# Recording both mixers of a two-layer encoder and ordering them with one list planner for all engines

## The chip, the cores and the metric

The kernel is one program on one NeuronCore of a Trainium2 chip. The metric is the device time of one execution in microseconds (us), lower is better. The engines named below are PE (TensorE matmul), DVE (VectorE), ACT (ScalarE), POOL (GpSimd) and SP (SyncE, which issues most weight loads). Each engine runs its own instructions in order and waits on semaphores for the others.

## The reference, cut to what matters

512 tokens of width 1024 go through two layers. Each layer is a mixer, a cross-attention to 256 memory tokens and a gated convolutional FFN; the mixers are what this case is about.

```python
# layer 0
proj = xn @ w_in                                   # 1024 -> 3080 columns
fox  = forgetting_attention(fq, fk, fv, log_f)     # 8 heads of 64: causal softmax(q k / 8 + F_q - F_k) v
diff = differential_attention(q1, q2, k1, k2, v)   # 4 heads: (softmax_1 - lam * softmax_2) v, chunk-causal
mixed = concat(fox, rms_norm(diff) * 0.8) @ w_out
x = x + mixed;  x = x + memory_cross_attention(...);  x = x + conv_ffn(...)
# layer 1
qk = silu(causal_conv(proj_qk));  h = mlstm_chunkwise(q, k, v, i, log_f)   # 4 heads, q/k 128, v 256
mixed = (rms_norm(h) * sigmoid(og)) @ w_out
x = x + mixed;  ...;  y = rms_norm(x)
```

## The kernel before, in words

Activations lie transposed in eight tiles of 128 x 512 (`x0` to `x7`). Almost every product is made in three passes (`mm3`, L388 to L390): both factors are split into a high and a low part, and high x high, high x low and low x high are summed in PSUM. So each weight block of 128 x 1024 is loaded by SP into a `raw` tile, cast by ACT to `wh` and subtracted by DVE to `wl`; three such sets of buffers rotate. One projection block is 24 matmuls of 512 columns. Four PSUM banks (`acc0` to `acc3`) hold projections, two `s` and two `w` banks hold scores, transposes and attention sums.

`mix0` writes the first mixer as items. A differential head is a q and a k projection (`p_qk`), eight score blocks with softmax (`p_soft`, L798 and L799: a matmul pair, a DVE reduction `sm`, an ACT exponential, a DVE reciprocal), transposes (`p_turn`, L831), a sum over values (`weigh`, L844), and an RMS norm whose per-token roots go through DRAM and back as a broadcast row (`p_far_norm`: POOL computes `y`, issues `roots<-y`, then `hrb<-roots`). A fox pair (two heads of 64) does the same with two heads side by side (`weigh`, L1068, 64 columns each); its bias rows come from `decays`, a running sum of the log forget gates that DVE and ACT compute, POOL sends to DRAM and then spreads over 128 partitions (`fb<-decays`); POOL masks them (`tb<-fb`). `p_memory` prepares the memory tokens for the cross-attention, `p_fill` computes blocks of its keys early, into a bank that stays held until the next stage, and `p_out` is the output projection, eight blocks over the eight mixed tiles.

`mix1` is the mLSTM likewise: gates (two scans, logs and exponentials on four rows), two value projections, and for each of four heads a q and a k block with a convolution of four taps and a tanh, two output gates, four score blocks, the row sums (`dens`, L2254), the sums over values (`nums`, L2275) and the norm.

Two planners stand in the file. `Plan` keeps one clock for PE and rough clocks for ACT and DVE: each item has a PE duration, a priority, resources and a `chain` of rough durations behind it. It picks the ready item of the lowest priority number and calls its function, which issues all of the item's instructions, those of DVE, ACT, POOL and SP among them, in that order. Both mixers are ordered by `Plan` alone: the instructions then go to the framework in the order of issue, and the framework, which knows their dependencies, orders each engine's list. `Sched` is finer: every instruction of every engine is a task with a duration, a latency, ring buffers that it takes and frees, and a due time; the engine with the earliest possible start goes next. `rest` (cross-attention and FFN of a layer) is ordered by `Sched`, and there `planned(True, 4)` chains the instructions of DVE, ACT, POOL and SP each to the one before by an ordering edge without a semaphore, so that the planned order is the order on the engine. All instructions of DVE, ACT, POOL and SP go through the helper at L310 and carry that line.

Of the kernel before, what the change touches and what calls it, by code (L numbers as in the profile page):

```python
# [31 lines left out]
DECAY_AT = 90.0  # L32
MEM_AT, MEM_STEP = (140.0, 100), (24.0, 16.0)
FILLS, FILL_AT, FILL_PRIO = 2, (210.0, 140.0), 99
# [41 lines left out]
class Item:  # L76
    def __init__(self, fn, dur, deps, prio, take, free, chain, pre, after, order, load, st):
# [8 lines left out]
class Plan:  # L86
# [11 lines left out]
    def add(self, fn, dur=0.0, deps=(), prio=None, take=(), free=(), chain=(), pre=(), after=0.0, order=(), load=(), st=None, soon=False):  # L98
        it = Item(fn, dur, [d for d in deps if d is not None], len(self.items) if prio is None else prio, take, free, chain, pre, after, order, load, st)
        it.n, it.soon = len(self.items), soon  # L100
        self.items.append(it)
        return it

    def run(self):
        todo = sorted(self.items, key=lambda i: (i.prio, i.n))
        eng, t = self.eng, self.t
        while todo:
# [27 lines left out]
            for e, d in pick.pre:  # L135
                eng[e] = max(eng[e], t - 4.0) + d
            t += pick.dur
# [28 lines left out]

class Task:
    def __init__(self, eng, dur, fn, deps, prio, take, free, lat, after):
        self.after = after
        self.eng, self.dur, self.fn, self.prio, self.lat = eng, dur, fn, prio, lat  # L170
        self.deps = [d for d in deps if d is not None]
        self.take, self.free = take, free
        self.end = None


WAIT = {"DVE": 0.4, "ACT": 0.3}
ONE, TWO, FORM, THEN = 4, 12, 10.0, (2, 1, 1)
OUT = (0, 4, 1, 5, 2, 6, 3, 7)

class Sched:  # L180
# [3 lines left out]
    def __init__(self, wait={}, **res):  # L184
        self.tasks, self.wait, self.held, self.ahead = [], wait, [], AHEAD
# [16 lines left out]
    def dues(self):  # L202
# [6 lines left out]
        for r, s in self.slots.items():  # L209
            takes = [(t, st) for t in self.tasks for q, st in t.take if q == r]  # L210
            if r == "acc":
                takes = [(None, st) for st in self.held] + takes
# [22 lines left out]

    def run(self):
        if self.wait:
            self.dues()
# [5 lines left out]
        for t in self.tasks:  # L244
            for r, _ in t.take:
                want[r].append(t)
# [3 lines left out]
        while any(todo.values()):  # L250
            best = None
            for e, ts in todo.items():
                able = []
                for t in ts[:120]:
                    at = max(t.after, -99.0 if e == "-" else now[e])
                    ok = True
                    for d in t.deps:
# [3 lines left out]
                        at = max(at, d.end + (0.0 if d.eng == e else d.lat))  # L261
                    if not ok:
                        continue
                    for j, (r, _) in enumerate(t.take):
                        if want[r][0] is not t:
# [14 lines left out]
            if e == "PE":  # L280
                idle += at - now[e]
            t.start, t.end = at, at + t.dur
            now[e] = t.end
            for r, st in t.take:
                want[r].pop(0)
# [10 lines left out]

class InOrder:
# [3 lines left out]
    def __init__(self, tc, engine):  # L301
        self.tc, self.engine = tc, engine
# [3 lines left out]
    def __getattr__(self, name):  # L306
        issue = getattr(self.engine, name)

        def call(*a, **k):
            i = issue(*a, **k)  # L310
# [7 lines left out]
    def follow(self, after=None):  # L318
        self.next = after or True


class Engines:
    def __init__(self, tc, names):
        self.nc = tc.nc
        self.chains = [InOrder(tc, getattr(tc.nc, n)) for n in names]
# [10 lines left out]

class Builder:
    def __init__(self, tc, t):
        self.tc, self.nc, self.t = tc, Engines(tc, ORDERED), t
# [12 lines left out]
    def til(self, pool, tag, shape=(P, 512), dtype=F32, bufs=None):  # L352
        return pool.tile(list(shape), dtype, tag=tag, name=self.nm(tag), bufs=bufs or 2)

# [47 lines left out]
    def p_proj(self, pl, src, xs, evac, chain, deps=(), kdeps=None, edeps=(), prio=None, n=SEQ, nk=KB8, order=None, etake=(), per=2, eorder=(), load=()):  # L402
# [5 lines left out]
        for c, e in zip(cuts, cuts[1:] + [nk]):  # L408
# [12 lines left out]
            for k in ks:  # L421
# [4 lines left out]
                pre=(("A", 0.12 * nk), ("D", 0.14 * nk)) if first else (), st=st,  # L426
            )
        return pl.add(lambda: evac(st["ps"]), 0, [last, *edeps], prio, take=etake, free=("acc",), chain=chain, order=eorder, load=load, st=st, soon=True)
# [92 lines left out]
    def p_out(self, pl, src, mixed, kdeps, gain, gi, order, prio, reload=False, order0=None):  # L521
# [3 lines left out]
        for m in range(KB8):  # L525
            e = self.p_proj(
                pl, src[m], mixed, lambda ps, m=m: self.xadd(m, ps, reload), (("D", 0.6),), kdeps=kdeps, order=order, prio=prio + m
# [192 lines left out]
    def split_rows(self, pool, *rows):  # L720

        t = pool.tile([P, SEQ], F32R, name=self.nm("rows"))
# [50 lines left out]
    def p_qk(self, pl, dq, dk, par, kdeps, edeps, prio):  # L773

        st = {}
        q = self.p_proj(
            pl, dq, self.xs, lambda ps: st.update(q=self.q_parts(ps)), (("D", 0.66), ("A", 0.52), ("D", 0.6), ("D", 0.6)), load=(("A", 0.52),),
# [3 lines left out]
            pl, dk, self.xs, lambda ps: st.update(k=self.k_parts(ps, par)), (("D", 0.6), ("A", 0.52), ("D", 0.6), ("D", 0.6)), load=(("A", 1.56),),  # L781
# [64 lines left out]

    def p_values(self, pl, src, edeps, prio, kdeps=None, ready=None):
# [28 lines left out]
    def mix0(self):  # L876
        nc, t, tc = self.nc, self.t, self.tc
        with tc.tile_pool(name="mix0", bufs=1, reuse_waits="tile") as mp:
            self.mp = mp
            self.kbt = [[mp.tile([P, 512], F32R, name=f"kb{s}{i}") for i in range(2)] for s in range(2)]  # L880
# [4 lines left out]
            sub8 = self.warm[:, 2:3]  # L885
            dmask = mp.tile([P, 512], F32, name="dmask")
            nc.vector.memset(dmask[:], 0.0)
            nc.vector.memset(dmask[0:64, 448:512], BIG)
            mh, ml = ([None if k in (2, 3) else mp.tile([P, SEQ], F32R, name=f"{n}{k}") for k in range(8)] for n in ("mh", "ml"))
# [4 lines left out]
            self.x = [self.xp.tile([P, SEQ], F32, name=f"x{k}", tag=f"x{k}") for k in range(KB8)]  # L894
# [74 lines left out]
            for h in range(4):  # L969
                p = 10 + 10 * h  # L970
                if h == 0:
                    v, ve = self.p_values(pl, t["dv"], [norm], p - 1, xk, [lambda: vw[1:], second])
                st, qk = self.p_qk(pl, t["dq"][h], t["dk"][h], h % 2, xk, [norm], p)
                pt = {}
                got = pl.add(lambda pt=pt: pt.update(t=self.til(mp, "pt", (P, 1536), bufs=3)), 0, qk, p + SOFT_PRIO, take=("pt",))
                ss, ts = [], []
                for i in range(4):
                    n = P * (i + 1)
                    bias = lambda n=n: dmask[:, 512 - n : 512]
                    r1, a1, b1 = self.p_soft(pl, st, 0, i, bias, qk, p + SOFT_PRIO)  # L980
                    r2, a2, b2 = self.p_soft(pl, st, 1, i, bias, qk, p + SOFT_PRIO)
# [9 lines left out]
                    c = pl.add(both, 0, [b1, b2], p + SOFT_PRIO, free=("e",), chain=(("D", 0.08), ("A", 0.1 + 0.45 * n / 512), ("D", 0.07 + 0.6 * n / 512)))  # L991
                    ss += [a1, a2]
                    ts.append(self.p_turn(pl, r1, i, pt, [c, got], p + SOFT_PRIO))
                pl.add(lambda: None, 0, ss, p + SOFT_PRIO, free=("qk",))
# [9 lines left out]
                w = pl.add(weigh, 2.14, ts + ve, p + SOFT_PRIO, take=("w", "ta"), free=("w", "pt"), chain=(("A", 0.5),))  # L1004
                used.append(w)
                if h == 3:
                    pl.add(lambda: None, 0, used, p + SOFT_PRIO, free=("v",))
                w = pl.add(lambda: None, 0, [w], p + SOFT_PRIO, chain=(("A", 0.52),))
# [6 lines left out]
                f = self.p_far_norm(pl, sq, 1.0 / P, EPS, (mp, "hrb", (P, SEQ), F32, 1), scaled, [w], p + SOFT_PRIO, chain=(("D", 0.66),), late=LATE)  # L1015
                kd[4 + h] = [pl.add(lambda: None, 0, [f], p + SOFT_PRIO, free=("ta",), chain=(("A", 0.52), ("D", 0.6)))]


            for p_ in range(4):
                p = 50 + 10 * p_  # L1020
                if p_ == 0:
                    v, ve = self.p_values(pl, t["fv"], [norm], p - 1, xk)
                    used = []
                st, qk = self.p_qk(pl, t["fq"][p_], t["fk"][p_], p_ % 2, xk, [norm], p)
# [3 lines left out]
                for s in range(2):  # L1028
# [9 lines left out]
                    got = pl.add(lambda pt=pt: pt.update(t=self.til(mp, "pt", (P, 1536), bufs=3)), 0, qk, p + SOFT_PRIO, take=("pt",))  # L1038
                    items.append((h, s, pt, fb, b, got, []))
                for i in range(4):  # L1040
                    n = P * (i + 1)
                    for h, s, pt, fb, b, got, ts in items:
# [8 lines left out]
                        r1, a1, b1 = self.p_soft(pl, st, s, i, bias, qk + [b], p + SOFT_PRIO)  # L1051
# [5 lines left out]
                        c = pl.add(norm1, 0, [b1], p + SOFT_PRIO, chain=(("D", 0.13 + 0.27 * n / 512),))  # L1057
                        ss.append(a1)
                        ts.append(self.p_turn(pl, r1, i, pt, [c, got], p + SOFT_PRIO))
                pl.add(lambda: None, 0, ss, p + SOFT_PRIO, free=("qk", "fb", "fb"))  # L1060
                def weigh(p_=p_, pts=[i[2] for i in items], v=v):
# [16 lines left out]
                    pl.add(weigh, 2.4, ts + ve, p + SOFT_PRIO, take=("w",), free=("w", "pt", "pt"), chain=(("A", 0.5), ("D", 0.6)))  # L1078
                )
                used += kd[p_]  # L1080
                if p_ == 3:
                    pl.add(lambda: None, 0, used, p + SOFT_PRIO, free=("v",))
            self.p_memory(pl, 0, MEM_AT[0], MEM_STEP[0], [g])
            self.p_fill(pl, 0, FILL_AT[0], FILL_PRIO, FILLS)
            self.p_out(pl, t["wo0"], lambda: (mh, ml), kd, "xat", 0, [4, 5, 6, 7, 0, 1, 2, 3], 100, True, self.memnorm)
            pl.run()
            self.plan = pl
# [52 lines left out]
    def p_fill(self, pl, layer, after, prio, blocks):  # L1140

        self.fills = []
        for b in range(blocks):
            st = {}
            last = None
            for m in (2 * b, 2 * b + 1):
                for k in range(0, KB8, 4):

                    def fn(m=m, k=k, st=st):
                        if k == 0:  # L1150
                            st["w"] = self.weight(self.t["xk"][layer, m])
                            if m % 2 == 0:
                                st["ps"] = self.acc_bank(st["banks"][0])
                        (wh, wl), (xh, xl) = st["w"], self.mems()
# [9 lines left out]
                        pre=(("A", 0.95), ("D", 1.14)) if first else (), st=st,  # L1164
# [937 lines left out]
    def mix1(self):  # L2102
        nc, t, tc = self.nc, self.t, self.tc
        H = 4
        with tc.tile_pool(name="mix1", bufs=1, reuse_waits="tile") as mp:
            self.mp = mp
            pl = Plan(s=2, w=2, at=2, q=2, wt=3)
# [391 lines left out]
```

## Time and profile before

| | us |
|---|---|
| median of 3 runs | 1406.71 |
| lowest, highest run | 1405.83, 1407.87 |
| the profiled execution, its device time | 1407.05 |
| its span from first to last instruction | 1404.9 |
| PE busy, DVE busy, ACT busy, POOL busy | 1390.2, 1186.4, 874.4, 146.8 |

The stages follow each other: the first mixer until about 255 us, the rest of layer 0 until about 680, the second mixer until about 932, the rest of layer 1 and the final norm until the end. A PE row in the timeline gives the start of a matmul and its modelled length. Matmuls are pipelined, so that the next one starts before the modelled end of the one before; the distance between two starts tells more than the busy time. The granted TensorE clock is 1.000 over the whole run.

### The profile page before, as it was taken

What the parts mean: (1) busy time and instruction counts of PE and PEld (TensorE: products, weight loads), DVE (VectorE), ACT (ScalarE), POOL (GpSimd) and SP (SyncE); (2) the same over time, 40 slices, a digit from 0 to 9 for tenths busy, and PEclk for the clock granted to TensorE, in tenths of its full rate; (3) what the DMA queues carried; (4) which work ended last, traced back from release to release, by engine and by line L of the source; (5) the groups of instructions that cost most, each with busy time, mean ns of one, the idle gap of its engine ahead of it and who ended that gap; (6) DMA issues with size and microseconds to landing.
All of it is one profiled execution on the core that took longest, in us unless ns stands there. A gap on an engine that the chain in (4) does not pass through costs nothing.

```text
span 1404.9 us, 23512 instructions
## 1 busy us (share of the span) xinstructions
PE 1390.2 (99%) x8876; PEld 1265.2 (90%) x8876; DVE 1186.4 (84%) x2042; ACT 874.4 (62%) x1486; POOL 146.8 (10%) x213
## 2 busy tenths in 40 slices
PE   9999999999999999999999999999999999999998
PEld 8888878899899999999888888989989999999997
DVE  7787786888799999999768876678878999999984
ACT  6797565666576665666456664456656866565555
POOL 0002230010011111011001120001000111110000
PEclk9999999999999999999999999999999999999999
DMA  6225324765567787674333332367464878776522
GB/s 207 91 53 154 117 68 151 246 188 158 158 145 191 211 199 187 151 200 106 86 108 105 129 98 83 120 188 240 136 185 114 196 201 204 182 185 168 154 66 81
DMA packets 80544, 211.06 MB, mean 150 GB/s; under 512 B 8640, under 2 KB 8640, under 8 KB 80432
## 3 DMA queue, kind: packets, MB, share of 16 engines
q1 hardware_dynamic: 63520, 165.02, 36.3%
q0 software_dynamic: 15904, 43.44, 17.7%
q8 instruction: 69, 1.13, 0.3%
q10 hardware_dynamic: 1008, 1.12, 0.2%
q14 instruction: 43, 0.35, 0.1%
HBM read 203.20 MB, written 6.34 MB: 149 GB/s over the span
## 4 chain that ended last, share of the span: by engine, by line
PE 85%; DVE 8%; ACT 3%; issue 2%; DMA 1%; POOL 1%; SPq 0%; POOLq 0%; DVEq 0%; ACTq 0%
PE acc L388 16%; PE acc L390 16%; PE acc L389 16%; PE w L388 4%; PE w L389 4%; PE w L390 4%; PE s L388 3%; PE s L390 3%; PE s L389 3%; PE acc L451 2%; PE acc L452 2%; PE acc L450 2%; DVE wl L310 1%; DVE qc L310 1%; PE w L2275 1%
## 5 line engine op out<-in xcount | busy, mean ns | idle before, releaser
L310 ACT CAST wh<-raw 128x1024 fp32r<-128x1024 f32 (+2 forms) x217 | 222.0, 1026 | 160.9 <-PE acc L389 76.4
L310 DVE TENSOR_TENSOR wl<-raw,wh 128x1024 fp32r<-128x1024 f32 (+2 forms) x217 | 259.6, 1198 | 39.2 <-ACT wh L310 37.9
L388 PE MATMUL acc<-xh,wh 128*128 128x256 f32 (+1 forms) x704 | 228.7, 325 | 0.0
L390 PE MATMUL acc<-xh,wl 128*128 128x256 f32 (+1 forms) x704 | 227.4, 323 | 0.5 <-DVE wl L310 0.5
L389 PE MATMUL acc<-xl,wh 128*128 128x256 f32 (+1 forms) x704 | 227.1, 323 | 0.0
L390 PEld LDWEIGHTS acc<-xh,wl 128*128 128x128 f32 x704 | 134.4, 191 | 9.3 <-DVE wl L310 0.9
L388 PEld LDWEIGHTS acc<-xh,wh 128*128 128x128 f32 x704 | 134.5, 191 | 7.6
L389 PEld LDWEIGHTS acc<-xl,wh 128*128 128x128 f32 x704 | 134.5, 191 | 7.5
L310 DVE SCALAR_TENSOR_TENSOR qc<-va,vec,qc 128x512 f32<-128x512 f32 x176 | 131.8, 749 | 6.9 <-ACT qc L310 4.0
L389 PE MATMUL acc<-f,k 128*128 128x256 f32 x336 | 92.5, 275 | 0.0
L390 PE MATMUL acc<-f,k 128*128 128x256 f32 x336 | 92.5, 275 | 0.0
L388 PE MATMUL acc<-f,k 128*128 128x256 f32 x336 | 92.5, 275 | 0.0
L310 ACT ACTIVATE qc<-va,vec 128x512 f32<-128x512 f32 x88 | 71.1, 812 | 19.2 <-DVE q L310 9.5
L388 PE MATMUL w<-q,wh 128*128 128x512 f32 x208 | 79.1, 380 | 0.6 <-ACT qc L310 0.6
L390 PE MATMUL w<-q,wl 128*128 128x512 f32 x208 | 78.9, 379 | 0.0
L389 PE MATMUL w<-q,wh 128*128 128x512 f32 x208 | 78.9, 379 | 0.0
L310 ACT ACTIVATE u<-acc 128x256 f32<-128x256 f32 x96 | 36.4, 379 | 68.1 <-PE acc L390 66.4
L390 PE MATMUL acc<-mem,wl 128*128 128x256 f32 (+1 forms) x236 | 73.8, 313 | 1.1 <-DVE wl L310 1.1
L388 PE MATMUL acc<-mem,wh 128*128 128x256 f32 (+1 forms) x236 | 73.9, 313 | 0.1
L389 PE MATMUL acc<-mem,wh 128*128 128x256 f32 (+1 forms) x236 | 73.7, 312 | 0.0
L310 DVE TENSOR_TENSOR x<-acc,x 128x512 f32<-128x512 f32 (+1 forms) x43 | 28.0, 653 | 47.2 <-PE acc L390 47.2
L310 ACT CAST k<-xe 128x512 fp32r<-128x512 f32 x84 | 51.0, 614 | 25.4 <-DVE xe L310 10.7
(414 smaller groups left out, 4207.0 us busy)
## 6 DMA issues: line engine op xcount, KB each, us to landing
raw<-in_up_dram SPq DMA_DIRECT2D x46, 512.0 KB, 4.3
raw<-in_down_dram SPq DMA_DIRECT2D x32, 512.0 KB, 4.6
sa<-in_up_dram SPq DMA_DIRECT2D x28, 512.0 KB, 5.1
sa<-in_up_dram POOLq DMA_DIRECT2D x28, 512.0 KB, 6.5
vb<-in_up_dram SPq DMA_DIRECT2D x42, 256.0 KB, 4.0
xe<-in_up_dram POOLq DMA_DIRECT2D x42, 256.0 KB, 4.8
raw<-in_wo_dram SPq DMA_DIRECT2D x16, 512.0 KB, 3.6
raw<-in_xk_dram SPq DMA_DIRECT2D x16, 512.0 KB, 3.9
```

Of the source, the lines that this page charges most:

```text
L310: i = issue(*a, **k)
L388: mm(out, wh, xh, start=first, stop=False, skip_group_check=parts)
L389: mm(out, wh, xl, start=False, stop=False, skip_group_check=parts)
L390: mm(out, wl, xh, start=False, stop=last, skip_group_check=parts)
L450: mm(ps, xh[k][:, ts], wh, start=(k == 0), stop=False)
L451: mm(ps, xh[k][:, ts], wl, start=False, stop=False)
L452: mm(ps, xl[k][:, ts], wh, start=False, stop=(k == 7))
L2275: nc.tensor.matmul(ps[:, lo:], vv[s][:, c], a[:], start=(s == 0), stop=(s == 3))
```

## The change

The items of both mixers still go through `Plan.run`, but their instructions are no longer issued there. A `Recorder` stands in front of the engines: each call becomes a `Task` of `Sched`, with a duration from a table by engine, operation and size (`cost`), with dependencies worked out from the tiles that it reads and writes (`Ref`, `View`, `touch`), and with the ring buffers of its tiles. The first 14 us of layer 0 are issued directly as before; everything later in the two mixers is recorded. Then `Sched` runs over all tasks twice: a first pass on the PE order of `Plan` (with a lead for softmax items, `EARLIES`), and a second pass in which PE tasks are ordered by the starts that the first pass gave, and the other engines' tasks by due times worked back from them. The result is issued with the ordering edges on for DVE, ACT, POOL and SP. A switch of the ACT table costs 1.3 us in the plan; a transfer that POOL issues costs 0.57 us on POOL and 2.0 or 3.6 us until it has landed, which also holds for a POOL instruction behind it that needs it.

Beside this the priorities of projections, softmax items and gates become lists of their own, the decay rows may be computed from 20 us of the plan's clock on instead of 90, the memory tokens are prepared from 110 and 70 instead of 140 and 100, and the fills may start from 86 and 28 instead of 210 and 140, the second one not before the last projection. `p_half`, which splits the fox values in two, is added but is not used, since `FV` has one entry. The instructions themselves stay the same.

```diff
-DECAY_AT = 90.0
-MEM_AT, MEM_STEP = (140.0, 100), (24.0, 16.0)
-FILLS, FILL_AT, FILL_PRIO = 2, (210.0, 140.0), 99
+DECAY_AT = 20
+MEM_AT, MEM_STEP = (110, 70), (16.0, 8.0)
+FILLS, FILL_AT, FILL_PRIO = 2, (86.0, 28.0), 99
+FILL_DUE, FILL_LAST = ((None, None), (None, None)), (1, 1)
...
+TABLES, TABLE = {AF.Exp: "exp", AF.Tanh: "exp", AF.Ln: "ln"}, 1.3
+PROJ = [10, 14, 36, 31, 52, 71, 79, 96]
+SOFT = [12, -6, 23.5, 21.5, 58.5, 51.5, 70.5, 87.5]
+FV = [42]
+EARLIES = [114.0, 72.0, 36.0, 2, 12.0, 78.0, 26, 33.0]
+PROJ1, SOFT1, NORM1 = [11, 8, 20, 37], [-19, -5.5, 32.5, 61], [24, 15.5, 24.5, -2.5]
+GATE1, V1 = [59, 72, 32, 95], [-20, 34]
+AGAIN = 1, 1
+AGAINS = {}, {"DVE": 0.4, "ACT": 0.3}, {}, {"DVE": 0.1, "ACT": 0.1}
+LEAD = {"SP": 8.0, "ACT": -0.1, "DVE": -2.2}, {"SP": 10.0, "ACT": 4.0, "DVE": 4.0}
+BEGIN, EARLY = (14.0, 0.0), 0.0
...
 class Sched:
+    def again(self, wait):
+        ...
+        self.run()
+        for t, (fn, dur) in zip(self.tasks, kept):
+            t.prio = t.start if t.eng == "PE" else 1e6 if t.eng == "-" else 1e5
+            t.fn, t.dur, t.end = fn, dur, None
...
-                        at = max(at, d.end + (0.0 if d.eng == e else d.lat))
+                        at = max(at, d.end + (d.same if d.eng == e else d.lat))
...
+            if t.table and t.table != self.table:
+                self.table, t.dur = t.table, t.dur + TABLE
...
+class Recorder:
+    def cost(self, eng, name, out, a, k):
+        if name == "dma_start":
+            return (0.0017 * n, 3.3) if eng == "sync" else (0.57, 2.0 if n < 512 or out.shape[0] < P else 3.6)
+        if eng == "tensor":
+            if name == "transpose":
+                return 0.109, 0.2
+            ...
+            return (max(0.11, MM * n / 512) if wide else max(0.22, 4 * MM * n / 512)) * (0.7 if "tile_position" in k else 1.0), 0.2
+        if eng == "vector":
+            two = 0.065 + 1.06e-3 * n
+            ...
+        if eng == "scalar":
+            d = 0.1 + 0.83e-3 * n + (0.07 if name == "copy" and n == 512 else 0.0)
+            ...
+        return {"affine_select": 0.14 + 0.85e-3 * n, "tensor_tensor": 1.3, "memset": 0.1}.get(name, 0.1), 0.25
+    def add(self, eng, issue, name, a, k):
+        ...
+            t = self.sc.add(E, dur, None, (), self.clock - self.early + (0.0 if E == "PE" else 3.0), lat=lat)
+            t.same = lat if name == "dma_start" else 0.12 if E != "PE" else 0.0
+            t.loose = self.it is not None and (self.it.prio > FILL_PRIO or self.it.late)
+    def run(self):
+        ...
+        if AGAIN[self.layer]:
+            sc.again(AGAINS[AGAIN[self.layer]])
+        sc.run()
+        self.b.nc.planned(False, 4)
...
 def mix0(self):
-                p = 10 + 10 * h
+                p, soft = PROJ[h], SOFT[h]
...
-                p = 50 + 10 * p_
+                p, soft = PROJ[4 + p_], SOFT[4 + p_]
...
-            self.p_fill(pl, 0, FILL_AT[0], FILL_PRIO, FILLS)
+            self.p_fill(pl, 0, FILL_AT[0], FILL_PRIO, FILLS, [qk[1].pe])
+            pl.rec = self.rec
             pl.run()
-            self.plan = pl
+            rec = self.rec
+            rec.run()
```

More of the change, by code (lines that the diff above doesn't have):

```diff
@@ L76, with __init__ @@
 class Item:
-    def __init__(self, fn, dur, deps, prio, take, free, chain, pre, after, order, load, st):
+    def __init__(self, fn, dur, deps, prio, take, free, chain, pre, after, order, load, st, due=None, behind=(), late=False):
+        self.due, self.behind, self.late, self.tasks = due, behind, late, []
         self.fn, self.dur, self.deps, self.prio, self.st = fn, dur, list(deps), prio, st
@@ L96, in __init__, with add @@
         self.res["acc"] = self.banks.values()
-    def add(self, fn, dur=0.0, deps=(), prio=None, take=(), free=(), chain=(), pre=(), after=0.0, order=(), load=(), st=None, soon=False):
-        it = Item(fn, dur, [d for d in deps if d is not None], len(self.items) if prio is None else prio, take, free, chain, pre, after, order, load, st)
+    def add(self, fn, dur=0.0, deps=(), prio=None, take=(), free=(), chain=(), pre=(), after=0.0, order=(), load=(), st=None, soon=False, due=None, behind=(), late=False):
+        it = Item(fn, dur, [d for d in deps if d is not None], len(self.items) if prio is None else prio, take, free, chain, pre, after, order, load, st, due, behind, late)
         it.n, it.soon = len(self.items), soon
@@ L209, in dues @@
         for r, s in self.slots.items():
-            takes = [(t, st) for t in self.tasks for q, st in t.take if q == r]
-            if r == "acc":
-                takes = [(None, st) for st in self.held] + takes
+            takes = [(t, st) for t in self.tasks for q, st in t.take if q == r and not t.loose]
+            takes = [(None, st) for st in (*self.had.get(r, ()), *(self.held if r == "acc" else ()))] + takes
             for (a, st), (b, _) in zip(takes, takes[len(s):]):
@@ L244, in run @@
         for t in self.tasks:
-            for r, _ in t.take:
+            for r, _ in t.take if not t.loose else ():
                 want[r].append(t)
@@ L309, in call @@
         def call(*a, **k):
-            i = issue(*a, **k)
+            if self.rec and not self.rec.issuing:
+                return self.rec.add(self.name, call, name, a, k)
+            i = issue(*map(real, a), **{w: real(v) for w, v in k.items()})
             if self.last is not None and (self.on or self.next):
@@ L318, in follow @@
     def follow(self, after=None):
-        self.next = after or True
+        if not self.rec:
+            self.next = after or True
 class Engines:
@@ L400, in proj, with p_proj @@
         return ps
[L402 removed]
+    def p_proj(self, pl, src, xs, evac, chain, deps=(), kdeps=None, edeps=(), prio=None, n=SEQ, nk=KB8, order=None, etake=(), per=2, eorder=(), load=(), behind=()):
         order = order or list(range(nk))
@@ L1138, in mems, with p_fill @@
         return [m[0] for m in self.mem], [m[1] for m in self.mem]
-    def p_fill(self, pl, layer, after, prio, blocks):
+    def p_fill(self, pl, layer, after, prio, blocks, behind=()):
         self.fills = []
```

430 lines of the change are left out of this document (366 added, 64 removed).

## The prediction

> **What bounds the kernel now.** I read the page's engine totals first, then the busy times by stage, then the PE timeline inside the mixers, and last the groups of PE instructions in the worst stretch.
>
> ```profile
> PE 1390.2 (99%) x8876; PEld 1265.2 (90%) x8876; DVE 1186.4 (84%) x2042; ACT 874.4 (62%) x1486; POOL 146.8 (10%) x213
> ```
>
> ```profile
> core 0: us, PE busy (x) PEld busy (x) DVE busy (x) ACT busy (x) POOL busy (x), PEclk, DMA share, GB/s
> 14.00:255.00 241.00, 237.32 (x1246) 199.39 (x1247) 184.05 (x465) 160.90 (x325) 32.86 (x56) 1.00 0.37 111
> 168.00:215.00 47.00, 44.97 (x254) 32.48 (x252) 37.22 (x124) 27.25 (x71) 12.27 (x24) 1.00 0.24 75
> 255.00:680.00 425.00, 423.83 (x3047) 401.17 (x3046) 392.32 (x621) 272.21 (x458) 45.22 (x54) 1.00 0.67 175
> 680.00:932.00 252.00, 250.44 (x1221) 215.19 (x1219) 182.68 (x275) 135.32 (x194) 22.89 (x43) 1.00 0.34 106
> ```
>
> PE is the bound, so only time in which PE does not start matmuls can be won. By busy time that is 3.7 us in the first mixer (241.00 - 237.32) and 1.6 us in the second (252.00 - 250.44), 5.2 us together. DVE is at 184 of 241 us (76%) in the first mixer and ACT at 161 (67%), so neither is full over the stage; in the stretch from 168 to 215 DVE is at 79%.
>
> The busy time hides the larger part, as two neighbours show:
>
> ```profile
> 59.63 0.38 PE L388 MATMUL acc<-xh,wh 128*128 128x512 f32 x1
> 59.85 0.38 PE L389 MATMUL acc<-xl,wh 128*128 128x512 f32 x1
> ...
> 168.03 0.60 PE L831 MATMUL w<-ident,x 128*128 128x128 f32 x4
> 168.39 0.46 PE L388 MATMUL acc<-mh,wh 128*128 128x512 f32 x1
> 168.69 0.38 PE L389 MATMUL acc<-ml,wh 128*128 128x512 f32 x1
> ...
> 172.21 2.37 PE L1068 MATMUL w<-pt,v 128*64 128x512 f32 x16
> 174.52 0.33 PE L831 MATMUL w<-ident,x 128*128 128x128 f32 x1
> ...
> 187.94 2.98 PE L1068 MATMUL w<-pt,v 128*64 128x512 f32 x16
> 190.85 0.33 PE L831 MATMUL w<-ident,x 128*128 128x128 f32 x1
> ```
>
> A 512-column matmul is 0.38 us long but the next starts after 0.22 us (59.85 - 59.63; 0.2155 over long runs), so a gap of up to 0.16 us never shows as idle. Four transposes and one such matmul take 0.66 us (168.69 - 168.03), hence 0.11 us a transpose. A fox sum of 16 matmuls takes 2.31 us at best (174.52 - 172.21) and 2.91 us another time (190.85 - 187.94). [...]
>
> ```profile
> L831 PE MATMUL w<-ident,x 128*128 128x128 f32 x68 | 11.8, 282 | 0.5 <-DVE pt L310 0.2 <-DVE x L310 0.2
> L388 PE MATMUL acc<-mh,wh 128*128 128x512 f32 x18 | 7.3, 408 | 0.0
> L1068 PE MATMUL w<-pt,v 128*64 128x512 f32 x16 | 6.5, 618 | 0.1
> L798 PE MATMUL s<-ka,qa 128*128 128x256 f32 x9 | 2.8, 313 | 0.4 <-DVE sm L310 0.4
> L798 PE MATMUL s<-ka,qa 128*128 128x512 f32 x6 | 2.5, 410 | 0.0
> L798 PE MATMUL s<-ka,qa 128*128 128x384 f32 x6 | 2.1, 348 | 0.3 <-DVE sm L310 0.3
> L388 PE MATMUL acc<-qa,wh 128*128 128x512 f32 x3 | 0.9, 415 | 0.7 <-ACT qa L310 0.7
> ```
>
> That is the stretch from 168 to 215. Work at full rate: 512 columns, 3 x 18 of `mh`, 3 x 6 of `qa` and `ka`, 2 x 6 scores and 1 more, 85 x 0.2155 = 18.3 us; scores of 384, 12 x 0.16 = 1.9 (0.16 taken as three quarters of 0.2155); 256 columns, 21 x 0.11 = 2.3 (half of it); transposes 68 x 0.11 = 7.5; four sums of ones, 0.4; all four fox sums, 4 x 2.31 = 9.2. Together 39.6 of 47.0 us: **7.4 us are lost**, and all four fox pairs are weighed here. They are bunched because their bias rows come late:
>
> ```profile
> 116.44 0.53 POOL L310 DMA_DIRECT2D decays<-tmp  x1 [27.25 <-DVE tmp L310]
> 118.50 0.54 POOL L310 DMA_DIRECT2D fb<-decays  x1 [1.53 <-DMA decays<-tmp]
> ```
>
> The other losses stand one by one:
>
> ```profile
> 90.41 0.38 PE L451 MATMUL acc<-wl,xh 128*128 128x512 f32 x1
> 91.18 0.43 PE L798 MATMUL s<-ka,qa 128*128 128x384 f32 x1 [0.40 <-DVE sm L310]
> ...
> 215.19 0.28 PE L389 MATMUL acc<-mem,wh 128*128 128x256 f32 x1
> 216.56 0.38 PE L390 MATMUL acc<-mem,wl 128*128 128x256 f32 x1 [1.09 <-DVE wl L310]
> ...
> 762.71 0.38 PE L390 MATMUL acc<-xh,wl 128*128 128x512 f32 x1
> 763.91 0.48 PE L388 MATMUL s<-q,k 128*128 128x512 f32 x1 [0.82 <-ACT k L310]
> ...
> 816.34 0.38 PE L390 MATMUL acc<-xh,wl 128*128 128x512 f32 x1
> 817.28 0.91 PE L547 MATMUL s<-ones,hsq 128*128 128x2 f32 x7 [0.56 <-DVE hsq L310]
> ```
>
> Step less full rate: 0.55 us at 90, 1.26 at 215 (a fill whose `wl` is not ready), 0.98 at 763, 0.72 at 816. With the smaller ones beside them, estimated as as much again at 90 to 93 and in the second mixer, there are some 10 us in the first mixer (7.4 + 1.26 + 1.3) and 3.5 us in the second. **Most to be won: 13.5 us.**
>
> **The change part by part.** Work on PE, DVE, ACT and in bytes stays as it is, so every term is an idle gap closed or opened. (1) The first 14 us are issued as before: 0. (2) The decay chain may run at 20 instead of 90 us of the plan. It is the same instructions at another time, hidden under the projections (DVE has 57 us free in the stage, 241 - 184); its effect is that the fox rows can be in place before the fox projections end, so the four pairs need not share 47 us. (3) The fills (two blocks of keys, 48 matmuls each of half width, 48 x 0.11 = 5.3 us) may start at 86 and the second is kept for the drain of the last pair. They are moved past projections on SP's queue; each brings two loads, two casts and two subtractions, 2 x 1.22 us on DVE. They take a PSUM bank earlier, so that projections have three instead of four. I cost this at 0 and name the cover: three banks of 5.2 us of work (24 x 0.2155) each. What was late at 215, the fill's `wl`, is planned with its load; late next is the last pair's `ml`. (4) The priorities interleave softmax with projections: that and the common order of all engines are what can close the 7.4 us.
>
> How much is closed I take from the stages that `Sched` orders already. There PE loses 1.2 us busy time (425.00 - 423.83) in 425 us, against 3.7 in 241 for the first mixer: 0.28% against 1.5%. By starts I estimate 3.1 us lost in that stage, in the ratio of 2.6 between starts and busy time that the mixers show (13.5 to 5.2). At that rate, 0.73 us in 100, the two mixers (241 + 210 us, the second from the end of the FFN's drain) keep 3.3 us and give 10.2. Mixers have longer chains (reduction, exponential, reciprocal, transposes, copies, and a trip through DRAM), so I let two thirds as much again stay: 5.5 us kept, **8.0 us won**, about 6 in the first mixer and 2 in the second. Ends for this term: all but what three fox sums vary (3 x 0.6 = 1.8), 11.7 us won; nothing won, 0; and a loss, which nothing excludes and rival C prices.
>
> (5) The plan's durations decide whether its order holds on the chip:
>
> ```profile
> L310 DVE TENSOR_TENSOR wl<-raw,wh 128x1024 fp32r<-128x1024 f32 x38 | 46.3, 1224 | 10.6 <-ACT wh L310 10.4
> L310 ACT CAST ka<-tmp 64x512 fp32r<-64x512 f32 x32 | 19.8, 617 | 1.6 <-DVE tmp L310 0.9
> L310 POOL TENSOR_SCALAR_AFFINE_SELECT tb<-fb 128x512 f32<-128x512 f32 x8 | 5.3, 671 | 7.5 <-DVE sm L310 7.5
> ```
>
> The plan has 1.15 us for the first (0.065 + 1.06 x 1.024), 0.595 for the second, 0.575 for the third: 6%, 4% and 14% short. With 24% of DVE free this shifts the plan, it does not break it: 0.07 us on 38 splits is 2.8 us over the whole mixer, against 57 free. (6) Table loads:
>
> ```profile
> 132.79 1.28 ACT L310 ACT_TABLE_LOAD   x1
> 134.08 0.40 ACT L310 ACTIVATE x<-x,sm 128x128 f32<-128x128 f32 x1
> ```
>
> From the load's start to the next exponential pass 1.29 us; the plan has 1.3. [...]
>
> (7) The chained order adds a wait of a kind: DVE and ACT can no longer let a ready instruction pass a late one. Behind a late broadcast row stand all later splits and softmax steps, and PE behind them after the three weight buffers are used up.
>
> **Sum.** The profiled execution: 1407.05 - 8.0 = 1399.05 us, its span 1404.9 - 8.0 = 1396.9. The median of the runs shown is 0.34 us below the profiled execution, so I say 1398.7 us.
>
> **The rivals.** (A) My forecast, own range 4 to 12 us won, 1394.7 to 1402.7.
>
> (B) The bunch stays: the last pairs' softmax is tied to DVE and to its own chain, and only the single gaps go (1.26 + 0.98 + 0.72 = 3.0 us): 1403.7, with a range of 1402.7 to 1406.7. For it: DVE at 79% and three `sm` waits in the bad stretch. Against: DVE has 57 us free in the stage and the rows could come 60 us earlier.
>
> (C) Slower: late landings block the chained queues.
>
> ```profile
> 142.62 5.12 DMA hrb<-roots
> ```
>
> The plan gives such a row 0.57 + 3.6 = 4.17 us from issue; this one, on the chain that ended last, took 5.12, 0.95 more. There are 21 broadcast rows in the mixers (8 `fb`, 7 `hrb`, 6 of the mLSTM). Where PE has no matmuls in hand for that long, each costs 0.95 us; nine uncovered rows eat the 8 us, and from then on the kernel is slower; with twelve it is 12 x 0.95 - 8.0 = 3.4 us slower, 1410.1. For it: DVE's subtractions stand behind such a row. Against: three weight buffers cover up to 5.2 us each.
>
> (D) The order comes out as it was in effect (the framework already sorted by readiness): 1406.7.
>
> **How the numbers follow.** A 0.70, B 0.17, C 0.10, D 0.03. About 0.2% (2.8 us) is what a measurement of this kernel can tell from no change. Faster by more: A whole, and half of B, 0.78. Within: half of B and D, 0.12. Slower: C, 0.10. The predicted time is A's, 1398.7 us. The range runs from A's lower end to just below D, 1394.5 to 1406.5: it leaves out C, D and the tails of A and B, about 0.2.
>
> **What would show it.** Right: the stretch before the output projection's end has PE starts without gaps, the fox sums lie spread over 100 to 215 us instead of 172 to 212, `decays` is issued before 60 us, the fill's `wl` wait of 1.09 us is gone, the second mixer loses its 0.82 us on `k`; the FFN stages keep their 425 us. Wrong: PE waits on DVE behind an `hrb` or `fb` landing (C), or the fox sums are still bunched with `sm` waits (B), or a gap at the border to the cross-attention, where the next stage's plan presumes the end of this one.

## The result and the profile after

The changed kernel takes 1397.84 us (median of 4 runs, 1397.16 to 1398.75) against 1406.84 us before: ratio 0.9936, 95% interval 0.9919 to 0.9954. It is 9.0 us faster.

The engine totals of the profiled execution after (1398.38 us): the instruction counts of PE, DVE and ACT stand as they were, the span is 8.6 us shorter. PE's busy time falls by 5.3 us at the same 8876 matmuls, since it counts small gaps between starts as busy (a 512-column row is 0.38 us long where the next starts after 0.22).

```profile
span 1396.3 us, 23543 instructions
PE 1384.9 (99%) x8876; PEld 1264.1 (91%) x8876; DVE 1187.7 (85%) x2042; ACT 874.1 (63%) x1486; POOL 149.7 (11%) x213
```

Where the time went is read from one matmul that every version has at the border of mixer and cross-attention, the first of the value block over the memory tokens (`acc<-wh,mem`). These are timeline rows of PE, start first; the kernel before, both layers:

```profile
253.06 0.38 PE L1386 MATMUL acc<-wh,mem 128*128 128x512 f32 x1
...
931.03 0.38 PE L1386 MATMUL acc<-wh,mem 128*128 128x512 f32 x1
```

The changed kernel (its PE calls go through the helper too, so that all carry L630):

```profile
247.30 0.38 PE L630 MATMUL acc<-wh,mem 128*128 128x512 f32 x1
...
922.18 0.38 PE L630 MATMUL acc<-wh,mem 128*128 128x512 f32 x1
```

The first mixer is 5.8 us shorter (253.06 - 247.30). From border to border it is 677.97 us before and 674.88 after, 3.1 us less, and that lies in the second mixer, for the FFN between stands as it was, as the busy times by stage of the changed kernel show:

```profile
14.00:249.30 235.30, 233.19 (x1246) 198.50 (x1246) 185.09 (x464) 160.64 (x324) 32.37 (x56) 1.00 0.37 114
165.00:212.00 47.00, 46.50 (x315) 37.24 (x314) 41.75 (x117) 29.50 (x69) 7.79 (x17) 1.00 0.42 136
249.30:674.30 425.00, 423.83 (x3047) 400.89 (x3046) 392.27 (x621) 272.23 (x458) 43.92 (x52) 1.00 0.67 175
674.30:923.00 248.70, 248.70 (x1220) 215.31 (x1218) 182.73 (x275) 134.64 (x193) 27.32 (x45) 1.00 0.34 108
```

The FFN stage has 423.83 of 425 us again, to the digit. In the second mixer PE is busy for all of its 248.70 us.

To count what busy time hides, I took the distance from each matmul's start to the next, less the full-rate step of its shape, and added that up. Before, 10.8 us are lost so in the first mixer after 14 us and 3.7 in the second; after, 5.3 and 0.6. That is 8.6 us won, as much as the span (the border rows give 8.9; the last stage is 0.3 longer). The four levels hang by up to a microsecond on the steps that one takes for the small shapes; the differences do not.

The worst stretch, 47 us that hold all four fox sums, now by groups of PE instructions:

```profile
L630 PE MATMUL acc<-mem,wh 128*128 128x256 f32 x64 | 11.8, 281 | 0.0
L630 PE MATMUL w<-ident,x 128*128 128x128 f32 x57 | 9.1, 277 | 0.2 <-DVE ml L630 0.2
L630 PE MATMUL acc<-mem,wl 128*128 128x256 f32 x32 | 8.8, 275 | 0.0
L630 PE MATMUL acc<-mh,wh 128*128 128x512 f32 x11 | 4.6, 419 | 0.0
L630 PE MATMUL acc<-xl,wh 128*128 128x512 f32 x12 | 4.5, 379 | 0.0
...
L630 PE MATMUL s<-ka,qa 128*128 128x256 f32 x8 | 2.4, 314 | 0.3 <-DVE sm L630 0.3
```

The work at full rate, in the prediction's manner: 74 of 512 columns (31 of `mh`, 35 projections, 8 scores) 15.9 us, 8 of 384 1.3, 112 of 256 12.3, 57 transposes 6.3, four fox sums 9.2: 45.0 of 47.0 us, 2.0 lost instead of 7.4. The 96 `mem` matmuls are the two fills; before, they came behind the stretch, from 215 on. The fox sums stand here (start, modelled length):

```profile
166.20 2.37 PE L630 MATMUL w<-pt,v 128*64 128x512 f32 x16
178.13 2.37 PE L630 MATMUL w<-pt,v 128*64 128x512 f32 x16
197.05 2.37 PE L630 MATMUL w<-pt,v 128*64 128x512 f32 x16
209.52 2.38 PE L630 MATMUL w<-pt,v 128*64 128x512 f32 x16
```

Before they began at 172, 188, 199 and 209; the last two, which the prediction does not show:

```profile
199.30 1.07 PE L1068 MATMUL w<-pt,v 128*64 128x512 f32 x2
...
209.09 2.85 PE L1068 MATMUL w<-pt,v 128*64 128x512 f32 x16
```

They are still bunched; what changed is what lies between them. All four now run at the best length. POOL's rows show that the bunch no longer waits for the decay rows: they leave at 38 instead of 116 us, and yet the first mask `tb` is made at 138. Before, it was made at 124 and did wait for them (first row; the others are the changed kernel's).

```profile
124.50 0.93 POOL L310 TENSOR_SCALAR_AFFINE_SELECT tb<-fb 128x128 f32<-128x128 f32 x1 [4.41 <-DMA fb<-decays]
...
37.71 0.72 POOL L630 DMA_DIRECT2D decays<-tmp  x1 [17.79 <-DVE tmp L630]
39.99 1.67 POOL L630 DMA_DIRECT2D fb<-decays  x3 [1.57 <-DMA decays<-tmp]
...
138.14 0.31 POOL L630 TENSOR_SCALAR_AFFINE_SELECT tb<-fb 128x128 f32<-128x128 f32 x1
```

The largest gap that is left in the mixers is this one, 1.07 us over the step: scores wait for DVE, which did two subtractions of 1.79 us together ahead of the reduction.

```profile
152.05 0.28 PE L630 MATMUL s<-kb,qa 128*128 128x256 f32 x1
153.23 0.35 PE L630 MATMUL s<-ka,qa 128*128 128x256 f32 x1 [0.91 <-DVE sm L630]
```

### The profile page after: what moved, and what is told of

Same layout as the page of the kernel before. It is cut to its first block, busy times and chain, and to the rows that moved or that the text cites. A ratio compares the mean times of both kernels' runs of the same rounds, so it can differ in the third digit from the quotient of the medians.

```text
span 1396.3 us, 23543 instructions
## 1 busy us (share of the span) xinstructions
PE 1384.9 (99%) x8876; PEld 1264.1 (91%) x8876; DVE 1187.7 (85%) x2042; ACT 874.1 (63%) x1486; POOL 149.7 (11%) x213
## 4 chain that ended last, share of the span: by engine, by line
PE 89%; DVE 7%; ACT 1%; issue 1%; DMA 1%; POOL 0%; POOLq 0%; SPq 0%; DVEq 0%; ACTq 0%
PE acc L630 61%; PE w L630 16%; PE s L630 12%; DVE qc L630 1%; DVE wl L630 1%; DVE x L630 1%; DVE va L630 1%; DVE sm L630 1%; DVE f L630 0%; DMA x<-in_x_dram 0%; DVE xe L630 0%; DVE k L630 0%; DMA roots<-y 0%; ACT qc L630 0%; DVE q L630 0%
## 5 line engine op out<-in xcount | busy, mean ns | idle before, releaser
L630 ACT CAST wh<-raw 128x1024 fp32r<-128x1024 f32 (+2 forms) x217 | 222.3, 1026 | 167.4 <-PE acc L630 109.6
L630 DVE TENSOR_TENSOR wl<-raw,wh 128x1024 fp32r<-128x1024 f32 (+2 forms) x217 | 260.0, 1199 | 38.9 <-ACT wh L630 37.6
L630 PE MATMUL acc<-xh,wh 128*128 128x256 f32 (+1 forms) x704 | 228.9, 325 | 0.0
L630 PE MATMUL acc<-xh,wl 128*128 128x256 f32 (+1 forms) x704 | 227.2, 323 | 0.5 <-DVE wl L630 0.5
L630 PE MATMUL acc<-xl,wh 128*128 128x256 f32 (+1 forms) x704 | 226.9, 322 | 0.0
L630 PEld LDWEIGHTS acc<-xh,wl 128*128 128x128 f32 x704 | 134.2, 191 | 9.9 <-DVE wl L630 1.3
L630 PEld LDWEIGHTS acc<-xh,wh 128*128 128x128 f32 x704 | 134.4, 191 | 7.5
L630 PEld LDWEIGHTS acc<-xl,wh 128*128 128x128 f32 x704 | 134.3, 191 | 7.4
L630 DVE SCALAR_TENSOR_TENSOR qc<-va,vec,qc 128x512 f32<-128x512 f32 x176 | 131.7, 749 | 7.1 <-ACT qc L630 4.2
L630 PE MATMUL acc<-f,k 128*128 128x256 f32 x1008 | 126.0, 275 | 0.0
L630 PE MATMUL w<-q,wh 128*128 128x512 f32 x416 | 123.9, 379 | 0.6 <-ACT qc L630 0.6
L630 PEld LDWEIGHTS acc<-f,k 128*128 128x128 f32 x1008 | 121.4, 192 | 1.6
L630 PE MATMUL acc<-mem,wh 128*128 128x256 f32 (+1 forms) x472 | 103.2, 313 | 0.0
L630 PEld LDWEIGHTS w<-q,wh 128*128 128x128 f32 x416 | 75.3, 190 | 9.7 <-ACT qc L630 1.0
L630 PEld LDWEIGHTS acc<-mem,wh 128*128 128x128 f32 x472 | 78.5, 191 | 4.7
L630 ACT ACTIVATE qc<-va,vec 128x512 f32<-128x512 f32 x88 | 71.1, 812 | 17.7 <-DVE va L630 9.0
L630 ACT ACTIVATE u<-acc 128x256 f32<-128x256 f32 x96 | 36.5, 380 | 69.7 <-PE acc L630 67.8
L630 PE MATMUL w<-q,wl 128*128 128x512 f32 x208 | 78.8, 379 | 0.0
L630 PE MATMUL acc<-mem,wl 128*128 128x256 f32 (+1 forms) x236 | 73.6, 312 | 0.0
L630 DVE TENSOR_TENSOR x<-acc,x 128x512 f32<-128x512 f32 (+1 forms) x43 | 28.1, 654 | 46.2 <-PE acc L630 46.2
L630 PE MATMUL acc<-f,wh 128*128 128x256 f32 x384 | 66.8, 275 | 0.0
L630 PE MATMUL s<-f,wh 128*128 128x256 f32 x384 | 66.7, 275 | 0.0
```

The source lines that it names most:

```text
L630: i = issue(*map(real, a), **{w: real(v) for w, v in k.items()})
```

## The experiments

Twelve kernels, each timed in five executions (e2, e5 and e6 in eleven) beside the kernel before. "First" is the start of the border matmul in layer 0, "second" the distance from it to the same matmul in layer 1, both from the profiled execution and as the difference to the kernel before (253.06 and 677.97).

| run | median us | ratio, 95% interval | first | second |
|---|---|---|---|---|
| the changed kernel | 1397.84 | 0.9919 to 0.9954 | -5.8 | -3.1 |
| e1, no second planning | 1418.55 | 1.0069 to 1.0097 | +7.0 | +5.0 |
| e2, first mixer only | 1404.53 | 0.9979 to 0.9997 | -7.1 | +4.4 |
| e3, second mixer only | 1411.00 | 1.0021 to 1.0046 | +6.7 | -3.1 |
| e4, no ordering edges | 1416.85 | 1.0066 to 1.0091 | +4.9 | +5.0 |
| e5, plan, old lists and dates | 1406.16 | 0.9994 to 1.0012 | +0.9 | -3.1 |
| e6, plan, old lists, new dates | 1408.19 | 1.0002 to 1.0020 | -3.8 | +3.5 |
| e7, decays from 60 | 1398.00 | 0.9931 to 0.9956 | -4.9 | -3.1 |
| e8, no table, no landing in the plan | 1413.51 | 1.0037 to 1.0064 | +5.2 | +1.4 |
| e9, no table in the plan | 1397.97 | 0.9930 to 0.9954 | -7.3 | -2.2 |
| e10, no landing in the plan | 1413.32 | 1.0043 to 1.0068 | +4.3 | +5.0 |
| e11, longer landing | 1397.47 | 0.9927 to 0.9955 | -7.0 | -2.9 |
| e12, one pass | 1397.92 | 0.9931 to 0.9956 | -7.2 | -3.1 |

A profile is one execution. Its device time exceeds its span by 1.8 us (e2) to 3.4 us (e12), and kernels with a median of 1398 us have first mixers up to 2.4 us apart, so differences of 2 us in one column are not read here. Three profiles lie at the end of what their kernel does: those of e5 and e6 are about the fastest of eleven executions (1405.53 and 1406.17 us), that of e10 is the slowest of five (1416.88 us).

**The plan against the lists: e1, e2, e3.** e1 lets the recorder issue everything directly, so that the new priorities and dates act through `Plan` alone; e2 and e3 do that in one mixer each.

```diff
-BEGIN, EARLY = (14.0, 0.0), 0.0
+BEGIN, EARLY = (1e9, 1e9), 0.0      # e2: (14.0, 1e9), e3: (1e9, 0.0)
...
+        self.start = 0.0
```

> Everything of the change but the second planning: new priorities, earlier decay rows, memory tokens and fills, issued directly in the order of Plan, with no ordering edges in the mixers. Theory 1 (the common order of all engines closes the gaps): within 2 us of the kernel before, 1405 to 1409 us, with the mixers as long as before. Rival theory 2 (earlier fox rows and new priorities un-bunch the softmax work by themselves): most of the 9 us gained, 1398 to 1401 us, and the fox sums spread from 165 to 212 us.

> The second planning in the first mixer alone; the second mixer is issued directly with its new priorities. Theory 1: the first mixer ends 5.8 us earlier as in the changed kernel and the second has no gain of its own, 1401.0 us (1400 to 1402.5). Theory 2: the second mixer gains its 3.1 us all the same, 1397.8 us.

> The second planning in the second mixer alone; the first is issued directly with new priorities and dates. Theory 1: only the 3.1 us of the second mixer, 1403.7 us (1402 to 1406). Theory 2: 1397.8 us, since the first mixer keeps its gain.

Neither theory foresaw e1: without the second planning the lists are 12 us slower than the kernel before. For the same reason e2 and e3 came out slower than the first theory's ranges (1404.53 against 1402.5 at most, 1411.00 against 1406). The waits of PE in the mixers (us in total, times, longest):

```profile
PE s L631 <- DVE sm L631: 3.8, 1, 3.8
PE w L631 <- ACT pt L631: 3.0, 3, 1.6
PE s L631 <- DVE at L631: 2.0, 1, 2.0
```

The longest of them lies behind a broadcast norm row. DVE stands 3.94 us for `hrb` with the reduction `sm` next on its list, and PE starts no matmul from 141.89 to 146.11:

```profile
145.09 0.75 DVE L631 SCALAR_TENSOR_TENSOR ta<-ta,warm,hrb 128x512 f32<-128x512 f32 x1 [3.94 <-DMA hrb<-roots]
...
146.11 0.58 PE L631 MATMUL s<-ka,qa 128*128 128x256 f32 x1 [3.84 <-DVE sm L631]
```

In all DVE stands 16.2 us for these rows in the mixers of e1 and 16.5 in e4, against 1.6 in the kernel before and 2.3 in the changed one. So part of what the plan is worth is what e10 isolates below.

The mixers act apart, within what one profile can tell: the first is 6 to 7 us shorter where it is planned (the changed kernel, e2) and 7 us longer where it is not (e1, e3), the second 3.1 us shorter or 4 to 5 us longer. The theory that the lists un-bunch the work by themselves is dead, and the other holds in direction: without the plan there is no gain. Against the same lists without it, the plan is worth 20.7 us (1418.55 - 1397.84).

**The ordering edges: e4.** The planned order is issued, but DVE, ACT, POOL and SP are not chained.

```diff
-            self.b.nc.planned(True, 4)
+            pass
```

> Both mixers planned and issued in the planned order, but without the ordering edges on DVE, ACT, POOL and SP, so that the framework may order them by its own rules. If the order of issue is enough: 1398 us as the changed kernel. If the framework reorders: part of the gain goes, 1400 to 1404 us, with new waits of PE on DVE or ACT in the mixers.

1416.85 us, beyond both expectations: nearly all of the plan's worth goes with the edges.

```profile
PE s L630 <- DVE sm L630: 4.8, 6, 1.5
PE acc L630 <- ACT v L630: 3.2, 2, 2.5
PE s L630 <- DVE at L630: 2.7, 2, 1.6
```

Waits of PE on DVE and ACT of the kind of e1 are back. That the framework sorts by its own rules there is the reading that fits; the two lists of instructions were not compared on the chip step by step.

**The plan without the lists: e5, e6.** Priorities as before and no leads; e5 has the old dates too, e6 the new ones.

```diff
-DECAY_AT = 20
+DECAY_AT = 90                       # e5 alone, with the old MEM_AT, MEM_STEP and FILL_AT
...
-PROJ = [10, 14, 36, 31, 52, 71, 79, 96]
-SOFT = [12, -6, 23.5, 21.5, 58.5, 51.5, 70.5, 87.5]
+PROJ = [10, 20, 30, 40, 50, 60, 70, 80]
+SOFT = [15, 25, 35, 45, 55, 65, 75, 85]
...
-EARLIES = [114.0, 72.0, 36.0, 2, 12.0, 78.0, 26, 33.0]
+EARLIES = [0.0] * 8
...
```

> The planner over all engines with the ordering edges, but with the priorities and the dates of the kernel before (decays from 90, memory tokens from 140 and 100, fills from 210 and 140) and no lead for softmax items. If the planned order itself closes the gaps: 1399 to 1403 us. If the new lists of priorities carry the gain once a plan holds them: 1405 us or more. From the runs so far (lists without a plan: 12 us slower; plan without edges: 10 us slower) I lean to the second at 0.6.

> As the run with the planner alone, but with the new dates of decays, memory tokens and fills. Beside it this tells what the dates are worth under a plan. If earlier fox rows matter: 3 us or more faster than the run with the old dates. If not: within 1.5 us of it.

e5 stands at the kernel before (1406.16 us). Its profiled execution has the shortest span of the eleven, 1402.5 us against a median of 1404.2. It shows a second mixer 3.1 us shorter without the lists and a first one 0.9 us longer; the median shows nothing of the 2.2 us between, so that the plan alone wins the second mixer's part is not shown. In the first mixer single gaps of before are still there, the fill's `wl` among them (waits of PE):

```profile
PE s L630 <- DVE sm L630: 2.8, 2, 1.4
PE acc L630 <- DVE wl L630: 1.4, 2, 1.1
```

With the new dates (e6) the first mixer is 3.8 us shorter in the profile, 4.7 less than in e5, and the second 3.5 longer. Of the 6.6 us between the second mixers 5.1 are one wait of PE for ACT (`v`, 3.38 us, until 895) and a stretch of half clock behind it (3.4 us long; half of it, 1.7 us, is lost by estimate). By the medians e6 is 2.0 us slower than e5, which neither expectation had. So in the time of the whole the lists without the plan lose and the plan without the lists gains nothing; both together gain 9 us. How lists and dates share the first mixer is open: the dates were moved together only, and by its profile e6 has 3.8 of the 5.8 us without the lists.

**Early decay rows: e7.**

```diff
-DECAY_AT = 20
+DECAY_AT = 60
```

> The changed kernel with the decay rows from 60 us of the plan's clock on instead of 20. My prediction's step (late rows bunch the fox pairs, early ones free them) wants some of the loss back: 1400 us or more. The rival, since the changed kernel masks its first fox row at 138 us although the rows landed before 45 us: rows at 60 are early enough, and it is 1398 us, within 1.5 us of the changed kernel.

1398.00 us, the changed kernel's time: the rival was right. The rows leave at 70 us there, and the sums begin at 165, 175, 190 and 207. A start at 90 under the new lists was not tried.

**What the plan has to know: e8, e9, e10, e11.** e8 takes both terms out, e9 and e10 one each, e11 makes landings longer. Only the order of the instructions changes by it.

```diff
-TABLES, TABLE = {...}, 1.3
+TABLES, TABLE = {...}, 0.0          # e8, e9
...
-            return (0.0017 * n, 3.3) if eng == "sync" else (0.57, 2.0 if n < 512 or out.shape[0] < P else 3.6)
+            return (0.0017 * n, 3.3) if eng == "sync" else (0.57, 0.25)     # e8, e10; e11: 2.6 and 3.8
```

> The changed kernel with a plan that knows nothing of table loads (0 instead of 1.3 us) nor of the landing of POOL's transfers (0.25 us instead of 2.0 or 3.6 us); on the chip both cost what they did. If these terms matter: DVE's list has the steps behind the broadcast rows too early, waits for them, and PE loses 2 to 8 us, 1400 to 1406 us. If the slack in DVE and the three weight buffers cover it: within 1 us of 1398 us.

> Only the table term out of the plan (0 instead of 1.3 us a switch); landings as in the changed kernel. There are four switches in the first mixer and three in the second, 9 us of ACT in all, of which the plan would know nothing. If the landing term made up the loss of the run without both: 1398 to 1400 us. If the table term did: 1405 us or more.

> Only the landing term out of the plan (0.25 instead of 2.0 or 3.6 us); the table term as in the changed kernel. In the run without both terms DVE waited 23 us for hrb rows in the mixers. If landing is the cause: 1406 to 1414 us, with the same waits of DVE. If it needs both: 1400 us or less.

> The changed kernel with the landing at 2.6 and 3.8 us, nearer to the rows of the trace (a roots row took 2.5 to 3.2 us until it had landed). If a truer plan is a better plan: the 1.7 us lost at 143 to 153 us go, 1396.5 us. Rival: the lists of priorities were fitted to the old durations, so any new set gives another order, 1396 to 1403 us by chance.

The landing term carries it: without it 1413.32 us, 15.5 us more than the changed kernel and more than e8's expectation had (1406 at most), and the table term adds nothing (1397.97 us without it; e8 and e10 take the same time). DVE's waits for the norm rows in the mixers, first the changed kernel, its only such wait of a microsecond or more, then e10:

```profile
DVE ta L630 <- DMA hrb<-roots: 2.3, 2, 1.8
```

```profile
DVE ta L630 <- DMA hrb<-roots: 14.2, 3, 5.4
DVE num L630 <- DMA hrb<-roots: 11.5, 2, 7.2
```

One of them in e10, from the timelines of POOL, DVE and PE. POOL issues the row at 202.89; DVE, whose list has the scaling of `ta` next, stands for 5.40 us, with the scaled `x` that PE's transposes need a few instructions behind it; PE starts nothing from 204.96 to 211.03.

```profile
202.89 0.54 POOL L630 DMA_DIRECT2D hrb<-roots  x1 [3.41 <-DVE x L630]
209.07 0.75 DVE L630 SCALAR_TENSOR_TENSOR ta<-ta,warm,hrb 128x512 f32<-128x512 f32 x1 [5.40 <-DMA hrb<-roots]
...
210.39 0.49 DVE L630 TENSOR_SCALAR x<-x,sm 128x512 f32<-128x512 f32 x1
...
204.96 0.38 PE L630 MATMUL acc<-mh,wl 128*128 128x512 f32 x1
211.03 1.08 PE L630 MATMUL w<-ident,x 128*128 128x128 f32 x4 [5.68 <-DVE x L630]
```

The waits of PE are not the whole loss: in three stretches of e10, 13.7 us together, the granted clock is half (last section), which makes by estimate some 6 (half of the time that PE works in them) of the 18.8 us between the two profiled spans (1415.1 and 1396.3).

e11 shows that landings nearer to the trace (1397.47 us) are not worth a measurable amount. It also speaks, though only for a small step, against a rival reading of e10, that any other duration upsets lists that were fitted to the old ones.

**The second pass: e12.**

```diff
-AGAIN = 1, 1
+AGAIN = 0, 0
```

> Only the first pass of the planner, with the order of PE by the clock of Plan and the leads, and no due times worked back from PE's planned starts. If the second pass carries gain: 1400 to 1406 us. If one pass is enough: 1398 us, within 1.5 us.

1397.92 us: one pass is enough. The span of its profiled execution, 1394.3 us, is 2.0 under the changed kernel's, but its other four are 1395.7 to 1396.0 us, where the changed kernel's lie too. No version beat the changed kernel by an amount that can be measured.

## Why the prediction was right, point by point

- **The sum.** Predicted 1398.7 us, 8.0 won; measured 1397.84 against 1406.84, 9.0 won. By stage about 6 and 2 were forecast, 5.8 and 3.1 came.
- **What can be won.** Counted by starts, 13.5 us were named; the full count gives 14.5. Busy time (5.2 us) is less than the gain itself, so the count by starts was needed.
- **What stays.** 5.5 us were to stay, 5.9 did (5.3 + 0.6). But the split failed: the forecast of 6 and 2 left 4 us in the first mixer and 1.5 in the second. The second, whose chains I called long, keeps 0.6 us, under the FFN's rate that I took as the floor (0.73 us in 100); the first keeps 5.3. That the two errors cancel is luck; the rate carried over from another stage foretold neither mixer.
- **Step 2, early decay rows un-bunch the fox pairs: wrong.** The rows come 79 us earlier and the sums begin 6 and 10 us earlier (the first two) or within 2 us of where they began; with the rows from 60 the time is the same (e7). The loss in the stretch went from 7.4 to 2.0 us with the bunch in place, and these 5.4 us are nearly all of the first mixer's gain.
- **Step 3, fills at cost 0: no cost showed, but the account leaves out what they cover.** 96 matmuls of theirs, 10.6 us at 0.11, moved into the stretch, work that PE can do while softmax is not ready. How much of the 5.4 us won there is theirs is not shown; all dates together are 4.7 us of the first mixer between the profiles of e5 and e6.
- **Step 4, the common order closes the gaps: right, but not alone.** The lists, which I named beside it without a price of their own, make the kernel 12 us slower without the plan (e1), and the plan gains nothing in the whole without them (e5, e6).
- **Steps 5 and 6.** Durations 4% to 14% short did not break the plan, and the table term changes nothing in the time (e9, 1397.97 us); ACT is busy for 160.9 of 241 us in the first mixer.
- **The signs.** `decays` is issued at 38 us, the waits of PE for the fill's `wl` (1.09 us) and for `k` (0.82 us) are gone, and the FFN keeps its 425 us. The fox sums did not spread.
- **Rival B** was right that the bunch stays and wrong in the time: the loss went all the same. **Rival C** named the right mechanism, chained queues behind broadcast rows, and the wrong size: not 0.95 us a row that is late by the plan, but single waits of DVE of 4.3 to 7.2 us when the plan has no landing at all (e10). The plan had the term, so it did not come. **D** fell with the result.

## What to carry to other kernels

Where the order on each engine is fixed, the plan must know the long waits: a transfer's landing left out of it cost 15.5 us here, a table load, a second pass and landings nearer to the trace nothing that could be measured. Priorities, plan and ordering edges were fitted together, and each without the others was no faster than before or slower, so such parts are to be judged together and not one by one. Where PE looks 99% busy, count the distances between its starts before saying that nothing is left, and read a bunch of work by what covers it, not by why it is bunched.

## What the runs showed of the hardware

The gap of e10 cost more than its length. After it the granted clock is about half until 216.8 us (windows of e10; the clock is the third number from the right), and 512-column matmuls start 0.43 us apart (213.61 - 213.18) instead of 0.2155:

```profile
211.00:214.00 3.00, 2.97 (x9) 2.57 (x10) 2.62 (x6) 0.90 (x2) 0.00 (x0) 0.50 0.30 55
214.00:217.00 3.00, 3.00 (x10) 2.04 (x8) 1.22 (x2) 0.00 (x0) 0.00 (x0) 0.54 0.69 225
217.00:220.00 3.00, 3.00 (x20) 1.70 (x20) 0.00 (x0) 0.57 (x1) 0.00 (x0) 1.00 0.49 162
...
213.18 0.63 PE L630 MATMUL acc<-mh,wh 128*128 128x512 f32 x1
213.61 0.63 PE L630 MATMUL acc<-ml,wh 128*128 128x512 f32 x1
```

So about 3 us came on top of the gap, an estimate: half of the 5.7 us that PE works in the stretch of half clock, which is 6.8 us long, from 209.9 to 216.8. Two more in the same run, from 844.7 and 885.7, are 3.4 us long each. The gap ahead of the last of them is short: PE starts nothing from 881.79 to 883.82, and eight products of two columns follow, which are little work.

```profile
883.82 1.05 PE L630 MATMUL s<-ones,hsq 128*128 128x2 f32 x8 [1.66 <-DVE hsq L630]
...
886.00:889.00 3.00, 3.00 (x14) 2.87 (x13) 2.73 (x7) 1.68 (x2) 1.34 (x1) 0.50 0.46 168
```

A part of the loss of e1, e3, e4, e6, e8 and e10 is of this kind, for the profile of each of these slower versions has such stretches: besides those of e10, two in e1 (6.8 and 3.4 us), one in e3 (6.8), one each in e4 and e6 (3.4) and four in e8 (3.4 each). The mean granted clock of these executions is 0.994 in e8 and e10, 0.995 in e1, 0.997 in e3, 0.998 in e4 and 0.999 in e6. The kernel before and the changed one (1.000 and 0.999) have none while PE has matmuls; e2, e5, e9, e11 and e12 stand at 0.999 and e7 at 0.998. The length of a gap alone does not decide: 2.50 us in e4 (until 854.87) and 2.35 us in e2 (until 781.23) left the clock at 1.00, where 1.66 us in e10 did not. What else decides is not shown here.

The stretches of half clock in these profiles are 3.4 us long or twice that, and gaps of 1.60 us (e4, until 820.76) and 1.66 us (e10) came ahead of one. The changed kernel's gaps in the mixers, 1.1 us at most after 14 us, left the clock at 1.00.
